# When the half-width sums of x are made in two MLP layers: beside the square products or inside the first quarter

## Chip, cores, metric

One core of a Trainium2 chip runs the whole program. The metric is device time in microseconds (us) of that core. The kernel before took 1035.24 us (median of 3 runs, 1034.46 to 1035.85).

## What is computed

The reference is an encoder of two layers on 512 tokens of width 1024, all in float32: a stick-breaking attention, then an MLP; a gated linear recurrence, then an MLP; a last norm. The change touches the two MLPs alone:

```
x = x + y                                  # behind the attention or the recurrence
h = rms_norm(x, norm_mlp[layer])
u = relu(h @ w1);  x = x + (u * u) @ w2    # w1: 1024 x 4096, w2: 4096 x 1024
```

## The kernel before, in words

Every float32 product is made of three products of halves: an operand is cast to a high half (`wh`, `xg`, `sh`, `bh`; a cast on ACT), and the low half (`wl`, `low`, `sl`, `bl`) is the difference, made on DVE. TensorE (PE) runs high by high, low by high and high by low.

An MLP works through the 4096 hidden features in four quarters of 1024. Quarter 0's first product is made plainly, as eight products of 24 matmuls (`squared(c)`, c from 0 to 7; this text calls them the square products). Everything else follows a scheme of seven products in place of eight on 2 x 2 blocks (`PRODUCTS`, P1 to P7): first the "down" step of quarter 0 (14 products, P1 0 to P4 1: name and half), then for the quarters 1 to 3 an "up" step and a "down" step of 14 products each. A loop in `run` goes through these products; `place(i)` numbers them in a cycle of 28, where 0 to 13 is up and 14 to 27 is down. Ahead of each product, `leave` reads the banks of the product before it (`collect`), and makes the halves of the weights for the product four further on (`prepare`: an addition on DVE or by an accumulating DMA from POOL, the cast `wh` on ACT, the difference `wl` on DVE).

The up steps need sums of blocks of x. With x cut into eight chunks, chunk k and chunk 4 + k make a pair (k from 0 to 3). Per pair, `sums_of_x(k)` scales both chunks by the norm's weights (two ACT instructions of 128x512) and makes four sums (four DVE instructions of 128x256, tile `x`); `halves_of_sums(k)` casts the halves (two ACT casts of 128x256 and one of 128x512) and takes the low halves (two DVE instructions of 128x256 and one of 128x512, tile `low`). So one pair is seven DVE and five ACT instructions. The first high half needs the place in `xgl` and the second the place in `xgh` that the plain x still occupies until the square products have used it. While that is so (`x_down` not yet called), a pair's two 128x256 casts go to a spare place (`bh` or `bl`, and `s3`), and `replace` copies them home later, two ACT casts per pair. A pair made later goes home directly.

What sets the order: PE's order is as written. Instructions of the other engines inside `run` keep the written order on ACT and on DVE (`Ordered`); those beside the square products are ordered by the framework's scheduler. Every engine takes its instructions in the order of its queue. Before, the first MLP made pairs 0 and 1 beside square products 4 and 5, pair 2 at the places 19 and 20, pair 3 at the places 24 and 25 of the first down step; the second MLP made pairs 0, 1, 2 beside the products 4, 5, 6 and pair 3 at the places 19 and 20. `replace` ran once, at place 21, for all pairs that lay aside. Helpers that record the order (line 776) stand for all of these instructions in the profile; the matmuls are at L236 to L238 (square products), L1107 (down) and L1012 (up).

Of the kernel before, what the change touches and what calls it, by code (L numbers as in the profile page):

```python
# [62 lines left out]
def hybrid_encoder(  # L63
# [40 lines left out]
    def f(ap):  # L104
        return ap.bitcast(F32)
# [28 lines left out]
    xgh, xgl = Chunks(0), Chunks(1)  # L134
# [629 lines left out]
    HS = S // 2  # L764
# [21 lines left out]
    class Mlp:  # L786
# [157 lines left out]
        def halves_of_sums(self, k):  # L944
# [14 lines left out]
            self.A.copy(self.s41[:, k, :], v)  # L959
            self.V.tensor_tensor(low, v, f(self.s41[:, k, :]), ALU.subtract)  # L960

        LOWER = {15: (0, 0), 16: (1, 0), 17: (0, 1), 18: (0, 2), 22: (1, 1), 23: (1, 2)}

        def lower(self, i, part):
# [14 lines left out]

        def replace(self):  # L980

            for k in list(self.s3):
                self.A.copy(xgh[:, k, HS:], f(self.s3[k]))
                here = self.s2(k)
                del self.s3[k]
                self.A.copy(self.s2(k), f(here))

        def slots_of(self, p):

# [154 lines left out]
        def run(self, first, between, end):  # L1144
# [13 lines left out]
            def place(i):  # L1158

                return (i + self.STEPS // 2) % self.STEPS  # L1160
# [8 lines left out]
            def add(i, ahead=1):  # L1169

                if i >= len(steps) or i in done or steps[i][3] not in ("P5", "P6"):
                    return
                *what, name = steps[i]
                far = what[0] == "down" and (name, what[2]) in FARS
                if ahead > (5 if far else 2 if name == "P5" else what[0] == "up"):
                    return
                if steps.index((*what, {"P5": "P1", "P6": "P5"}[name])) in made:
                    done.add(i)

                    self.added(unit(i), name, far=far)  # L1180
# [51 lines left out]
            def leave(i):  # L1232

                ahead = i + 4
                if i < 0:
                    return
                kind, q4, p, name = steps[i]
                bank = sums[kind, q4, p if kind == "up" else 0][self.PRODUCTS[name][3]]
                if kind == "down":
                    if q4 == 0 and place(i) == 21:  # L1240
                        self.replace()
                    if p:
                        self.collect(name, 0, bank[0])
                    if steps[min(ahead, len(steps) - 1)][0] == "down":
                        add(ahead, 0)
                    if p:
                        self.collect(name, 1, bank[1])
                    prepare(ahead)
                    if later and place(i) > 15:
                        later.pop()()  # L1250
                    if q4 == 0:
                        x_down(FRONT, ASIDE)
                        if place(i) in self.LOWER:
                            self.lower(*self.LOWER[place(i)])

                        k = ({19: 2, 20: 2, 24: 3, 25: 3}, {19: 3, 20: 3})[self.layer].get(place(i))
                        if k:
                            (self.sums_of_x if place(i) in (19, 24) else self.halves_of_sums)(k)
                    return
                u, three = us[p], bank.rearrange("p (i n) -> p i n", i=2)  # L1260
                keep = {"P1": 0, "P6": 1, "P5": 2, "P7": 3}.get(name)
                if keep is not None:

                    self.A.copy(u[keep], three)
                at, x, y, op = {
                    "P3": (1, three, u[1], ALU.subtract),
                    "P7": (2, u[2], u[3], ALU.subtract),
                    "P2": (0, u[0], three, ALU.add),
                    "P4": (3, three, None, None),
                }.get(name, (None,) * 4)  # L1270
                if op:
                    self.V.tensor_tensor(u[at], x, y, op)
                if name == "P4":
                    def fourth(u=u, three=three, p=p):
                        self.A.activation(u[3], three, AF.Relu)
                        self.square(u[3])
                        if p:
                            last_sums(u, self.SUMS[:2])
                        else:
                            self.sums(p, slice(0, 2))  # L1280

                    if p:
                        fourth()
                    else:
                        later.append(fourth)
                elif later:
                    later.pop()()
                prepare(ahead)
                if op:
                    def rest(u=u, at=at):  # L1290
                        self.A.activation(u[at], u[at], AF.Relu)
                        self.square(u[at])
                        if p:
                            self.split_slot(p, u[at], at)

                    if p and name == "P3":
                        later.append(rest)
                    else:
                        rest()
                    if name == "P2" and not p:  # L1300
                        self.split(p, slice(0, 2), slice(0, 3), slice(0, 3))
                elif name == "P4" and p:
                    last_sums(u, self.SUMS[2:3])
                    self.split_slot(p, u[2], 5)
                    later.append(lambda: last_sums(u, self.SUMS[3:]))
                    waiting[:] = [(p, u[j], 3 + j) for j in (0, 1, 3)]
                elif name in ("P5", "P6") and p:
                    n = ("P5", "P6").index(name)
                    self.split(0, n, slice(0, 4), slice(3, 7))
# [36 lines left out]
        def quarters(self, between, end):  # L1346
            for c in range(C - 1):
                self.squared(c)
                p, i = c // 4, c % 4 // 2
                if c % 2:  # L1350
                    self.split(p, i, slice(0, 3), slice(0, 3))
                    self.sums(p, i)
                    self.split(p, i, slice(0, 4), slice(3, 7))
                if c == 0:
                    units = self.from_down(0)
                    self.load(units, *self.FROM_UP)
                if c < 2:

                    for n in range(4 * c, 4 * c + 4):
                        self.sq.chunk(n, x[n], e=V)  # L1360
                if c == C - 2:
                    self.rr = self.sq.inv_squares(self.bank())
                between(c)

                k = c - 4
                if k in range(2 + self.layer):
                    with tc.issue_after(self.squares.ins):
                        self.sums_of_x(k)
                        self.halves_of_sums(k)
            self.run(units, between, end)  # L1370
            self.blocks.close()
# [460 lines left out]
```

## Time and profile before

| what | value |
|---|---|
| runs | 1034.46, 1035.24, 1035.85 us |
| the profiled execution's own time | 1034.89 us |
| its span in the profile | 1033.2 us |
| PE busy | 1022.3 us (99%) |
| DVE busy | 862.9 us (84%) |
| ACT busy | 713.5 us (69%) |
| granted PE clock | 0.999 |

The span is the time from the first to the last instruction in the profile; 1.7 us of the execution lie around it. Times below are us from the span's start. In a timeline row the first number is the start, the second the duration of the row (of all its instructions, where xN says more than one), then engine, line, operation, output<-input; what stands in brackets is the engine's idle time before the row and what ended it.

### The profile page before, as it was taken

The page shows a single profiled execution, that of the slowest core. Times are in us where ns is not written, and L with a number is a line of the kernel's source. Part 1 is how long each engine was busy: PE and PEld are TensorE (multiplying, and loading weights), DVE is VectorE, ACT ScalarE, POOL GpSimd, SP SyncE. Part 2 cuts the span into 40 slices and gives each one's busy share as a digit, 9 for nine tenths or more (in the row PEclk, how much of TensorE's full clock was granted, in tenths as well). Part 3 has the DMA queues.
Part 4 walks back from the last instruction along what each step waited for, and adds up shares of the span by engine and source line. Part 5 has one row for each costly group of instructions (what it writes and reads, how often), then busy time and mean ns, then how long its engine had stood idle before and what let it go on. Part 6 is the DMA issues. An engine that isn't in the chain of part 4 may idle for free.

```text
span 1033.2 us, 15885 instructions
## 1 busy us (share of the span) xinstructions
PE 1022.3 (99%) x5868; PEld 892.2 (86%) x5868; DVE 862.9 (84%) x1152; ACT 713.5 (69%) x1104; POOL 174.6 (17%) x235
## 2 busy tenths in 40 slices
PE   9999999999999999999999999999999999999997
PEld 7888888888888988988988888888888988988986
DVE  6988787847789699799799889984689899798898
ACT  6777676836778674774765689964777774874866
POOL 0444444420010010010011210300000010010012
PEclk9999999999999999999999999999999999999999
DMA  7745454537546667677683464452436677677663
GB/s 233 220 121 143 107 154 103 153 108 279 143 82 183 167 154 196 164 158 191 162 233 83 132 179 122 119 202 83 102 80 185 164 163 189 165 159 195 165 125 105
DMA packets 52700, 159.41 MB, mean 154 GB/s; under 512 B 6672, under 2 KB 7952, under 8 KB 52624
## 3 DMA queue, kind: packets, MB, share of 16 engines
q1 hardware_dynamic: 41376, 119.35, 35.8%
q0 software_dynamic: 10528, 38.28, 22.3%
q8 instruction: 46, 0.75, 0.3%
q10 hardware_dynamic: 720, 0.79, 0.2%
q14 instruction: 30, 0.25, 0.1%
HBM read 137.41 MB, written 4.19 MB: 137 GB/s over the span
## 4 chain that ended last, share of the span: by engine, by line
PE 89%; DVE 4%; ACT 3%; issue 2%; DMA 1%; POOL 0%; SPq 0%; DVEq 0%; ACTq 0%; POOLq 0%
PE ps_t L1107 13%; PE ps_acc L1012 8%; PE ps_z L1012 7%; PE ps_acc L1107 7%; PE ps_acc L236 5%; PE ps_acc L238 5%; PE ps_acc L237 5%; PE ps_o L1012 4%; PE ps_z L1107 3%; PE ps_t L236 3%; PE ps_t L237 3%; PE ps_t L238 3%; PE ps_o L236 2%; PE ps_o L237 2%; PE ps_o L238 2%
## 5 line engine op out<-in xcount | busy, mean ns | idle before, releaser
L776 ACT CAST wh<-b 128x1024 fp32r<-128x1024 f32 x168 | 174.1, 1050 | 112.5 <-DVE b L776 73.9
L776 DVE TENSOR_TENSOR wl<-b,wh 128x1024 fp32r<-128x1024 f32 x168 | 204.2, 1221 | 45.4 <-ACT wh L776 44.7
L1089 POOL DMA_DIRECT2D b<-in_w_dn x40 | 35.0, 876 | 352.0 <-DVE b L776 265.6
L236 PE MATMUL ps_acc<-xg,wh 128*128 128x512 f32 x200 | 81.6, 408 | 0.0
L1012 PE MATMUL ps_z<-xg,wh 128*128 128x256 f32 x384 | 79.0, 277 | 0.8 <-ACT u L776 0.8
L238 PE MATMUL ps_acc<-xg,wh 128*128 128x512 f32 x200 | 78.3, 392 | 0.0
L237 PE MATMUL ps_acc<-xg,wl 128*128 128x512 f32 x200 | 78.3, 391 | 0.0
L231 DVE TENSOR_TENSOR wl<-raw,wh 128x512 fp32r<-128x512 f32 (+2 forms) x70 | 62.2, 914 | 15.0 <-ACT wh L229 14.8
L600 DVE TENSOR_TENSOR_SCAN scan<-keep,later 128x128 f32<-128x128 f32 (+1 forms) x64 | 59.5, 933 | 16.2 <-ACT keep L590 9.9
L776 ACT ACTIVATE u<-u 128x512 f32<-128x512 f32 x100 | 63.1, 632 | 9.5 <-DVE u L776 7.7
L229 ACT CAST wh<-raw 128x512 fp32r<-128x512 f32 (+2 forms) x70 | 50.6, 758 | 23.9 <-PE ps_acc L238 7.3
L1012 PE MATMUL ps_z<-xg,wl 128*128 128x256 f32 x240 | 66.4, 277 | 0.0
L1012 PEld LDWEIGHTS ps_z<-xg,wh 128*128 128x128 f32 x384 | 62.8, 188 | 1.2 <-ACT u L776 1.0
L1012 PE MATMUL ps_acc<-xg,wh 128*128 128x256 f32 x288 | 61.6, 278 | 1.2 <-ACT u L776 1.2
L1089 POOL DMA_DIRECT2D b<-in_w_up x24 | 20.9, 870 | 241.8 <-DVE b L776 90.5
L604 POOL TENSOR_TENSOR w<-w,scan 128x128 f32<-128x128 f32 (+1 forms) x64 | 51.4, 805 | 54.4 <-DVE scan L600 51.4
L776 DVE TENSOR_TENSOR b<-b,b 128x1024 f32<-128x1024 f32 x48 | 58.7, 1224 | 1.3
L776 DVE TENSOR_TENSOR u<-u 128x512 f32<-128x512 f32 (+1 forms) x92 | 54.9, 597 | 2.6 <-ACT u L776 1.1
L1012 PE MATMUL ps_acc<-low,wh 128*128 128x256 f32 x192 | 53.2, 277 | 0.1
L1012 PE MATMUL ps_acc<-xg,wl 128*128 128x256 f32 x192 | 53.2, 277 | 0.0
L776 ACT CAST wh<-raw 128x1024 fp32r<-128x1024 f32 x46 | 48.0, 1045 | 6.9 <-PE ps_acc L1107 6.9
L1107 PE MATMUL ps_t<-wh,bh 128*128 128x512 f32 x126 | 49.4, 392 | 0.4 <-DVE c L776 0.4
(383 smaller groups left out, 3277.1 us busy)
## 6 DMA issues: line engine op xcount, KB each, us to landing
b<-in_w_dn SPq DMA_DIRECT2D x48, 512.0 KB, 4.6
b<-in_w_dn POOLq DMA_DIRECT2D x40, 512.0 KB, 5.5
b<-in_w_up SPq DMA_DIRECT2D x36, 512.0 KB, 4.6
b<-in_w_up POOLq DMA_DIRECT2D x24, 512.0 KB, 5.5
raw<-in_w_m SPq DMA_DIRECT2D x16, 512.0 KB, 4.3
raw<-in_w_dn SPq DMA_DIRECT2D x16, 512.0 KB, 4.6
raw<-in_w_in SPq DMA_DIRECT2D x16, 512.0 KB, 4.6
raw<-in_w_qk SPq DMA_DIRECT2D x12, 512.0 KB, 3.7
```

Source lines behind the costliest of these rows:

```text
L229: A.copy(wh[:, k, :], raw[:, k, :])
L231: V.tensor_tensor(wl[:, k, :], raw[:, k, :], f(wh[:, k, :]), ALU.subtract)
L236: PE.matmul(ps, wh, ah, start=start, stop=False)
L237: PE.matmul(ps, wl, ah, start=False, stop=False)
L238: PE.matmul(ps, wh, al, start=False, stop=stop)
L600: V.tensor_tensor_scan(sc[:, S - n : S][:, ::-1], keep[:, :n][:, ::-1], later[:, S - n :][:, ::-1], 1.0, ALU.mult, ALU.max,)
L604: G.tensor_tensor(wt, wt, sc[:, S - n + 1 : S + 1], ALU.mult)
L776: ins = getattr(self.e, name)(*args, **kwargs)
L1012: PE.matmul(ps[:, i * HS : (i + 1) * HS], m, y, start=new and i == k == n == 0, stop=i == 1 and k == C // 2 - 1 and n == 2, skip_group_che ...
L1089: G.dma_start(out=unit[b].rearrange("p j n -> p (j n)"), in_=unit["src"](to), accum_op=ALU.add)
L1107: PE.matmul(ps, m, y[:, jj, cols], start=first and n == 0, stop=last and n == 2, skip_group_check=not new,)
```

## The change

Three things move. In the first MLP pair 2 is made beside square product 6, and pair 3 takes over the places 19 and 20; the places 24 and 25 make none. In the second MLP pairs 0 and 1 are both made beside product 4, pair 2 beside product 5 and pair 3 beside product 6; the down step makes none. `replace` copies one pair at a time, at the places 19, 21, 24 and 25 while one lies aside: three pairs in the first MLP, four in the second, one more than before in each.

```diff
+        REPLACE = 19, 21, 24, 25
...
         def replace(self):
-            for k in list(self.s3):
-                self.A.copy(xgh[:, k, HS:], f(self.s3[k]))
-                here = self.s2(k)
-                del self.s3[k]
-                self.A.copy(self.s2(k), f(here))
+            k = min(self.s3)
+            here = self.s2(k)
+            self.A.copy(xgh[:, k, HS:], f(self.s3.pop(k)))
+            self.A.copy(self.s2(k), f(here))
...
-                    if q4 == 0 and place(i) == 21:
+                    if q4 == 0 and self.s3 and place(i) in self.REPLACE:
                         self.replace()
...
-                        k = ({19: 2, 20: 2, 24: 3, 25: 3}, {19: 3, 20: 3})[self.layer].get(place(i))
-                        if k:
-                            (self.sums_of_x if place(i) in (19, 24) else self.halves_of_sums)(k)
+                        if self.layer == 0 and place(i) in (19, 20):
+                            (self.sums_of_x, self.halves_of_sums)[place(i) - 19](3)
...
-                k = c - 4
-                if k in range(2 + self.layer):
+                for k in ({4: (0,), 5: (1,), 6: (2,)}, {4: (0, 1), 5: (2,), 6: (3,)})[self.layer].get(c, ()):
                     with tc.issue_after(self.squares.ins):
                         self.sums_of_x(k)
                         self.halves_of_sums(k)
```

Three places show how the queues change. The first is DVE in the first MLP, at the end of the first down step (`c_` are the collected outputs, `wl` low halves of weights, `b_` weight blocks, `x` and `low` the pair's sums and low halves). Before:

```order
L776 SCALAR_TENSOR_TENSOR c_3134<-ps_t,rr,c_3134 128x512 x2
L776 TENSOR_TENSOR wl<-b_3728,wh 128x1024
L776 TENSOR_TENSOR b_3728<-b_3728,b_3730 128x1024
L776 TENSOR_TENSOR x<-x 128x256 x4
L776 SCALAR_TENSOR_TENSOR c_3131<-ps_z,rr,c_3131 128x512 x2
L776 TENSOR_TENSOR wl<-b_3728,wh 128x1024
L776 TENSOR_TENSOR b_3728<-b_3728,b_3732 128x1024
L776 TENSOR_TENSOR low<-x,xg 128x256 x2
L776 TENSOR_TENSOR low<-x,s_3138 128x512
L776 TENSOR_TENSOR wl<-b_3728,wh 128x1024
```

The same place of the change:

```order
L776 SCALAR_TENSOR_TENSOR c_3134<-ps_t,rr,c_3134 128x512 x2
L776 TENSOR_TENSOR wl<-b_3745,wh 128x1024
L776 TENSOR_TENSOR b_3745<-b_3745,b_3747 128x1024
L776 SCALAR_TENSOR_TENSOR c_3131<-ps_z,rr,c_3131 128x512 x2
L776 TENSOR_TENSOR wl<-b_3745,wh 128x1024
L776 TENSOR_TENSOR b_3745<-b_3745,b_3749 128x1024
L776 TENSOR_TENSOR wl<-b_3745,wh 128x1024
```

The seven instructions of pair 3 have left the queue between the weights of the first up step.

The second place is ACT in the second MLP, from the end of the square products into the first down step (`sh` are high halves of the squares `u`, `s_` and `bl` places of the pairs' high halves, `ps_acc` the bank of square product 7). Before:

```order
L776 CAST sh<-u 128x1024
L776 CAST bl<-x 128x256
L776 CAST s_7356<-x 128x512
L776 ACTIVATE u<-ps_acc 128x512
L776 ACTIVATE u<-u 128x512
L776 CAST sh<-u 128x768
L776 CAST wh<-b_7427 128x1024
L776 CAST wh<-raw 128x1024
L776 CAST sh<-u 128x1024
L776 CAST wh<-b_7427 128x1024
```

The same place of the change:

```order
L776 ACTIVATE u<-ps_acc 128x512
L776 ACTIVATE u<-u 128x512
L776 CAST bl<-x 128x256
L776 CAST sh<-u 128x1024
L776 CAST sh<-u 128x768
L776 CAST wh<-b_7430 128x1024
L776 CAST wh<-raw 128x1024
L776 CAST s_7359<-x 128x512
L776 CAST sh<-u 128x1024
L776 CAST wh<-b_7430 128x1024
```

Before, `sh` and the two casts of pair 2 stood ahead of the reading of `ps_acc`; now `sh` and the same two casts of pair 3 stand behind it.

The third place is DVE in the second MLP, the same stretch. Before:

```order
L776 TENSOR_TENSOR sl<-u,sh 128x1024
L776 TENSOR_TENSOR low<-x,bl 128x256
L776 TENSOR_TENSOR low<-x,s_7356 128x512
L776 TENSOR_TENSOR sl<-u,sh 128x768
L776 TENSOR_TENSOR wl<-b_7427,wh 128x1024
L776 TENSOR_TENSOR u<-u 128x256 x4
L776 TENSOR_TENSOR wl<-raw,wh 128x1024
L776 TENSOR_TENSOR b_7427<-b_7427,b_7429 128x1024
L776 TENSOR_TENSOR sl<-u,sh 128x1024
L776 TENSOR_TENSOR wl<-b_7427,wh 128x1024
```

The same place of the change:

```order
L776 TENSOR_TENSOR sl<-u,sh 128x1024
L776 TENSOR_TENSOR sl<-u,sh 128x768
L776 TENSOR_TENSOR wl<-b_7430,wh 128x1024
L776 TENSOR_TENSOR u<-u 128x256
L776 TENSOR_TENSOR low<-x,s_7359 128x512
L776 TENSOR_TENSOR u<-u 128x256 x3
L776 TENSOR_TENSOR wl<-raw,wh 128x1024
L776 TENSOR_TENSOR b_7430<-b_7430,b_7432 128x1024
L776 TENSOR_TENSOR sl<-u,sh 128x1024
L776 TENSOR_TENSOR wl<-b_7430,wh 128x1024
```

The low halves that stood between the two `sl` now stand ahead of the first, and one 128x512 `low` has come in between the sums of `u`.

## The prediction

> **What bounds the kernel.** First the page's list of busy times, then the page of PE's waits.
>
> ```profile
> span 1033.2 us, 15885 instructions
> PE 1022.3 (99%) x5868; PEld 892.2 (86%) x5868; DVE 862.9 (84%) x1152; ACT 713.5 (69%) x1104; POOL 174.6 (17%) x235
> ...
> PE ps_acc L1012 <- ACT u L776: 1.2, 1, 1.2
> ...
> PE ps_z L1012 <- ACT u L776: 0.8, 1, 0.8
> ```
>
> PE sets the time: nothing that the change does to ACT or DVE counts unless PE waits less or more for it. The change leaves PE's instructions and their order as they are. Two of its few named waits are single events in an up step (L1012), for ACT. So I compare steps that have the same work, in the timeline of PE, by the starts of their first matmuls.
>
> ```profile
> 291.03 0.39 PE L1107 MATMUL ps_t<-wh,bh 128*128 128x512 f32 x1
> ...
> 329.93 0.28 PE L1012 MATMUL ps_acc<-xg,wh 128*128 128x256 f32 x1
> ...
> 371.65 0.39 PE L1107 MATMUL ps_t<-wh,bh 128*128 128x512 f32 x1
> ...
> 757.78 0.39 PE L1107 MATMUL ps_t<-wh,bh 128*128 128x512 f32 x1
> ...
> 796.80 0.28 PE L1012 MATMUL ps_acc<-xg,wh 128*128 128x256 f32 x1
> ...
> 834.98 0.39 PE L1107 MATMUL ps_t<-wh,bh 128*128 128x512 f32 x1
> ```
>
> L1107 to L1012 is the first down step, L1012 to L1107 the first up step. The up step takes 41.72 us in the first MLP (329.93 to 371.65) and 38.18 in the second (796.80 to 834.98), with the same matmuls. **3.54 us** are lost in the first MLP's alone, and the difference in work is that pair 3 is made there at the places 24 and 25, just ahead. The first down steps take 38.90 and 39.02 us.
>
> **Term 1: the first MLP's up step.** The timelines of DVE, POOL and ACT show the path of that loss.
>
> ```profile
> 327.23 1.79 DVE L776 TENSOR_TENSOR x<-x 128x256 f32<-128x256 f32 x4
> 328.94 1.40 DVE L776 SCALAR_TENSOR_TENSOR c<-ps_z,rr,c 128x512 f32<-128x512 f32 x2
> ...
> 332.65 0.75 DVE L776 TENSOR_TENSOR low<-x,xg 128x256 fp32r<-128x256 f32 x2
> 333.51 0.69 DVE L776 TENSOR_TENSOR low<-x,s 128x512 fp32r<-128x512 f32 x1
> 334.11 2.36 DVE L776 TENSOR_TENSOR wl<-b,wh 128x1024 fp32r<-128x1024 f32 x2
> ```
>
> ```profile
> 335.69 0.86 POOL L1089 DMA_DIRECT2D b<-in_w_up  x1 [6.93 <-DVE wl L776]
> ```
>
> ```profile
> 800.67 0.86 POOL L1089 DMA_DIRECT2D b<-in_w_up  x1 [5.00 <-DVE wl L776]
> ```
>
> ```profile
> 343.29 2.00 ACT L776 CAST wh<-b 128x1024 fp32r<-128x1024 f32 x2 [3.93 <-DMA b<-in_w_up]
> ```
>
> Pair 3 holds DVE from 327.23 to 328.94 and from 332.65 to 334.11: 3.17 us in front of the `wl` that has to be made before POOL may add to that block in place. POOL issues that addition 5.76 us after the step's first matmul (335.69 less 329.93), against 3.87 in the second MLP (800.67 less 796.80). ACT then stands idle for 3.93 us until it lands, with everything queued behind that cast: the next `wh`, the reading of the banks. Those are the 1.2 and 0.8 us for which PE waits. The change takes all seven DVE instructions away here. ACT gets two casts of pair 2 at place 24, against two scalings and three casts that go. Nothing else differs from the second MLP's step, so I take its 38.18 us: **-3.54 us**. The bounds are -2.0 (the two named waits alone) and -3.54.
>
> The load of x[7] back from memory waits for pair 3 and moves ahead with it on SP's queue. It stands there between loads of up weights and finds its chunk free by then; I count it at nothing, because the products that need those weights are a step away.
>
> **Term 2: the first MLP's first down step.** Pair 2 comes in beside product 6, and `replace` is spread. A pair costs DVE 3.17 us as above when each sum waits for the last. Between other instructions it costs less: two of 128x256 in 0.75 us means one every 0.34, the 128x512 holds the queue for 0.60 (333.51 to 334.11), so 6 x 0.34 + 0.60 = 2.64 us. The stretches it has to fit into, in the view by windows (PE, PEld, DVE, ACT, POOL busy):
>
> ```profile
> 285.60:301.00 15.40, 15.40 (x68) 12.70 (x69) 11.93 (x23) 9.55 (x14) 0.86 (x1) 1.00 0.11 27
> 743.60:767.60 24.00, 24.00 (x112) 19.97 (x111) 21.83 (x41) 18.17 (x30) 1.03 (x2) 1.00 0.26 56
> ```
>
> In the first MLP DVE has 15.40 - 11.93 = 3.47 us free, and ACT 5.85. The pair fits. In the queue of ACT the first collecting read of `ps_t` now stands ahead of an `sh` cast, where before it stood behind:
>
> ```profile
> 298.28 0.68 ACT L1121 ACTIVATE c<-ps_t,rr 128x512 f32<-128x512 f32 x1
> ```
>
> At most its 0.68 us is then in front of the weights of P5 1, for which PE waits at this place; bounds 0 and 0.7. The read comes only a little later than the cast before it ends anyway, so **+0.1 us**. The two copies at place 19 stand ahead of a weight cast, and two fewer stand at place 21: by then ACT has done the same four, so nothing is added there, and the extra two at place 24 fall into ACT's wait for DVE.
>
> **Term 3: the second MLP's first down step.** Here DVE has 24.00 - 21.83 = 2.17 us free for the same 2.64 to 3.17, and ACT's order is worse: reading product 7's bank now stands ahead of both an `sh` and a `bl` cast. I walk the queues from the end of product 7 on, with the old durations.
>
> ```profile
> 752.37 0.63 ACT L776 ACTIVATE u<-u 128x512 f32<-128x512 f32 x1
> 752.90 1.33 ACT L776 ACTIVATE x<-x,colt 128x512 f32<-128x512 f32 x2
> ...
> 756.37 1.05 ACT L776 CAST sh<-u 128x1024 fp32r<-128x1024 f32 x1
> 757.32 0.40 ACT L776 CAST bl<-x 128x256 fp32r<-128x256 f32 x1
> 757.62 0.62 ACT L776 CAST s<-x 128x512 fp32r<-128x512 f32 x1
> 758.14 0.59 ACT L776 ACTIVATE u<-ps_acc 128x512 f32<-128x512 f32 x1
> 758.76 0.63 ACT L776 ACTIVATE u<-u 128x512 f32<-128x512 f32 x1
> ```
>
> ```profile
> 757.45 1.23 DVE L776 TENSOR_TENSOR sl<-u,sh 128x1024 fp32r<-128x1024 f32 x1
> 758.59 0.42 DVE L776 TENSOR_TENSOR low<-x,bl 128x256 fp32r<-128x256 f32 x1
> ...
> 760.29 0.96 DVE L776 TENSOR_TENSOR sl<-u,sh 128x768 fp32r<-128x768 f32 x1 [0.49 <-ACT sh L776]
> 761.24 1.23 DVE L776 TENSOR_TENSOR wl<-b,wh 128x1024 fp32r<-128x1024 f32 x1
> 762.38 1.80 DVE L776 TENSOR_TENSOR u<-u 128x256 f32<-128x256 f32 x4
> 764.10 1.22 DVE L776 TENSOR_TENSOR wl<-raw,wh 128x1024 fp32r<-128x1024 f32 x1
> 765.23 1.22 DVE L776 TENSOR_TENSOR b<-b,b 128x1024 f32<-128x1024 f32 x1
> ...
> 767.62 2.36 DVE L776 TENSOR_TENSOR wl<-b,wh 128x1024 fp32r<-128x1024 f32 x2
> ```
>
> ```profile
> 768.90 0.50 PE L1107 MATMUL ps_acc<-wl,sh 128*128 128x512 f32 x1
> ```
>
> Product 7's last matmul ends at about 757.95, where the next product has started (757.78). ACT: reading the bank, 0.62 to the next start (758.14 to 758.76); the square, 0.53 (752.37 to 752.90); `bl`, 0.30 (757.32 to 757.62); so `sh` starts at 759.40 and ends 1.05 later, 760.45. DVE: `sl` 1.14 (757.45 to 758.59), `sl` 0.95 (760.29 to 761.24), `wl` 1.14 (761.24 to 762.38), so the sums of `u` begin at 763.7, not 762.38. Up to `wl<-raw` they take 1.72 (762.38 to 764.10) and 0.48 more for the `low` between them (0.60, and the 0.34 before it in place of 0.46). From there to the last `wl`, by way of the addition and ACT's cast, it is 3.52 as before (764.10 to 767.62). That `wl` starts at 763.7 + 2.20 + 3.52 = 769.4, not at 767.62: 1.8 us later. It is the weight of P5 1, and the PE row above starts within 0.1 us of its end: PE has no slack there. So **+1.8 us**; the bounds are 0.5 (2.64 less 2.17, all holes used) and 3.17 (none used).
>
> The Trainium skill, "VectorE: DVE Perf Modes", section "The DRAIN you can't avoid", says that the next DVE instruction does not start until the pipe of the one before is empty. By it, the six spacings on DVE in this walk would be full durations, some 0.1 us longer each; the sum would be worse by about 0.5 us, near 1033.5. The rows speak against it (`low` starts at 758.59, 0.09 ahead of the end of `sl`, and two `low` fit in 0.75), as does that page's later section, "Two Vector instructions with no wait between them", by which an instruction that isn't held starts earlier.
>
> Behind this point the second MLP gains: no pair is made at the places 19 and 20 any more. PE's row at the end of that step shows what its seven DVE instructions cost:
>
> ```profile
> 791.24 0.47 PE L1107 MATMUL ps_t<-wh,bh 128*128 128x512 f32 x1 [0.23 <-DVE c L776]
> ```
>
> With the wait, the matmul's stretched time (0.47, against 0.39) and the same in the one before it, that is about 0.5 us, and some 0.1 in smaller places. All DVE work behind place 20 is 3.17 us earlier relative to PE, far more than this lateness: **-0.6 us**. Eight copies instead of six stand on ACT, two of them at each of four places; ACT has room there for 0.6 each.
>
> **The sum** against the profiled execution (1034.89 us: 1033.2 span and 1.7 around it): -3.54 + 0.1 + 1.8 - 0.6 = -2.2, so 1032.7. The median of the three runs is 0.35 higher than that execution: **1033.0 us**.
>
> **Rivals.**
>
> *The second MLP hides its pair.* If the holes of 2.17 us can be used nearly in full and ACT reads product 7's bank without holding back `sh`, term 3 is 0.5 and the sum -3.5: 1031.7. For it speaks that ACT has 5.8 us free in that stretch; against it, that the walk begins at PE's own end of product 7, which no hole can move. Chance 0.13.
>
> *The up step is relieved only in part.* The accumulating DMA shares its time with loads that SP issues; if it lands late again, ACT's wait shrinks by the 1.9 us by which it is issued earlier, but the second wait (0.8 us and its stretched neighbours, 1.1) stays. Then term 1 is -2.4 and the result 1034.1. Trainium skill, "DMA: Bandwidth & Descriptors", section "Issuing engines are not separate DMA queues": DMAs of all issuers run on the same 16 engines and interleave. This trace cannot separate them, but the same additions land in the second MLP beside the same loads and PE doesn't wait. Chance 0.15. The same time comes out if term 3 is at its upper bound of 3.17 (1034.4): another 0.12.
>
> *Slower: the pair's own chain runs in series.* A pair goes back and forth between ACT and DVE: two scalings (1.33), four sums (1.79), the casts (0.40, 0.40, 0.62), the lows (0.75, 0.69): 6.0 us if the two in-order queues wait for each other at every step. Less the holes this is 6.0 - 3.47 = 2.5 us in the first MLP and 6.0 - 2.17 = 3.8 in the second, and PE waits for both: -3.54 + 2.5 + 3.8 - 0.6 = +2.2, so 1037.4. It decides once the pair takes DVE more than its free time in the two stretches, with DVE idle inside the pair. Against it: the scheduler has put a pair's steps between other instructions. Chance 0.11.
>
> **How the numbers follow.** The forecast has 0.49, with its own range of 1031.9 to 1034.1. A measurement of this kernel can tell about 0.2% from no change, 2.07 us: below 1033.17 is faster, above 1037.3 slower. The forecast lies right at the first line, so I give 0.30 of its chance to faster and 0.19 to the same; the first rival is faster, the partial ones the same, and the last slower. Together: faster 0.43, same 0.46, slower 0.11. The range leaves out the slower rival and little below: 1031.3 to 1035.6.
>
> **What would show it.** Right: the first MLP's up step at 38.2 us and ACT's idle time of 3.93 us before that cast gone; the second MLP's first down step at about 40.2 us, with a PE wait of about 1.8 us at the matmul `ps_acc<-wl,sh` for DVE `wl`; no wait for DVE `c` at that step's end. Wrong: an up step over 39 us, or a down step in the first MLP over 39.5; PE waits beside the square products, where it has none now, would mean that the pair in series is the case.

## The result, and the profile after

The changed kernel takes **1033.39 us** (median of 15 runs, 1031.86 to 1034.14), against 1034.84 us for the kernel before on the same chips (15 runs, 1034.46 to 1039.22). The ratio is 0.9978, with a 95% interval of 0.9970 to 0.9986: 1.4 to 3.1 us faster. The medians lie 1.45 us apart; the ratio agrees with that of the means, which gives 2.2 us, and one run of 1039.22 makes 0.3 us of it. The forecast was 1033.0, or 2.2 us faster. The profiled execution took 1033.58 us.

The page's first lines, and then the page of PE's waits, of the changed kernel:

```profile
span 1031.9 us, 15893 instructions
...
PE 1022.2 (99%) x5868; PEld 892.6 (87%) x5868; DVE 862.0 (84%) x1152; ACT 715.8 (69%) x1108; POOL 169.8 (16%) x235
```

```profile
PE ps_acc L1107 <- DVE wl L776: 0.7, 2, 0.5
...
PE ps_z L1107 <- DVE wl L776: 0.3, 1, 0.3
PE ps_t L1107 <- DVE c L776: 0.3, 1, 0.3
...
PE ps_t L1107 <- DVE wl L776: 0.2, 1, 0.2
```

The two waits of 1.2 and 0.8 us for ACT in the up step (L1012) have left the list, and new ones for `wl` in a down step (L1107) have come. The starts of the same steps as before, in PE's timeline:

```profile
291.83 0.39 PE L1107 MATMUL ps_t<-wh,bh 128*128 128x512 f32 x1
...
330.92 0.28 PE L1012 MATMUL ps_acc<-xg,wh 128*128 128x256 f32 x1
...
369.31 0.39 PE L1107 MATMUL ps_t<-wh,bh 128*128 128x512 f32 x1
...
755.25 0.39 PE L1107 MATMUL ps_t<-wh,bh 128*128 128x512 f32 x1
...
795.39 0.28 PE L1012 MATMUL ps_acc<-xg,wh 128*128 128x256 f32 x1
...
833.56 0.39 PE L1107 MATMUL ps_t<-wh,bh 128*128 128x512 f32 x1
```

| step | before | after | difference | forecast |
|---|---|---|---|---|
| first MLP, first down | 38.90 | 39.09 | +0.19 | +0.1 |
| first MLP, first up | 41.72 | 38.39 | -3.33 | -3.54 |
| second MLP, first down | 39.02 | 40.14 | +1.12 | +1.8 - 0.6 |
| second MLP, first up | 38.18 | 38.17 | -0.01 | 0 |

The steps add up to -2.03. The two profiled executions differ by 1.31 only, mainly because the first MLP's down step begins 0.80 later after the change (291.83 for 291.03). It begins between 290.1 and 292.9 in the traces of this study, and the differences arise ahead of 250 us, in the attention, which no kernel here changes. So the steps below are compared within the traces, and the times only where they differ by more than this.

### The profile page after: what moved, and what is told of

Same layout as the page of the kernel before. It is cut to its first block, busy times and chain, and to the rows that moved or that the text cites. A ratio compares the mean times of both kernels' runs of the same rounds, so it can differ in the third digit from the quotient of the medians.

```text
span 1031.9 us, 15893 instructions
## 1 busy us (share of the span) xinstructions
PE 1022.2 (99%) x5868; PEld 892.6 (87%) x5868; DVE 862.0 (84%) x1152; ACT 715.8 (69%) x1108; POOL 169.8 (16%) x235
## 4 chain that ended last, share of the span: by engine, by line
PE 90%; DVE 4%; ACT 3%; DMA 2%; issue 1%; SPq 0%; ACTq 0%; DVEq 0%
PE ps_t L1107 15%; PE ps_acc L1012 10%; PE ps_z L1012 8%; PE ps_acc L1107 7%; PE ps_acc L236 5%; PE ps_acc L238 5%; PE ps_acc L237 5%; PE ps_o L1012 5%; PE ps_z L1107 4%; PE ps_t L237 2%; PE ps_t L236 2%; PE ps_t L238 2%; PE ps_o L236 2%; PE ps_o L237 2%; PE ps_o L238 2%; PE ps_t L622 2%
## 5 line engine op out<-in xcount | busy, mean ns | idle before, releaser
L1012 PE MATMUL ps_z<-xg,wh 128*128 128x256 f32 x384 | 78.7, 277 | 0.0
L1012 PE MATMUL ps_z<-xg,wl 128*128 128x256 f32 x240 | 66.3, 276 | 0.0
L1012 PEld LDWEIGHTS ps_z<-xg,wh 128*128 128x128 f32 x384 | 62.8, 188 | 0.1
L1012 PE MATMUL ps_acc<-xg,wh 128*128 128x256 f32 x288 | 61.4, 277 | 0.0
L1012 PE MATMUL ps_acc<-xg,wl 128*128 128x256 f32 x192 | 53.1, 276 | 0.0
L1012 PE MATMUL ps_acc<-low,wh 128*128 128x256 f32 x192 | 53.0, 276 | 0.0
L1107 PE MATMUL ps_t<-wh,bh 128*128 128x512 f32 x126 | 49.2, 390 | 0.3 <-DVE c L776 0.3
```

The source lines that it names most:

```text
L1012: PE.matmul(ps[:, i * HS : (i + 1) * HS], m, y, start=new and i == k == n == 0, stop=i == 1 and k == C // 2 - 1 and n == 2, skip_group_che ...
L1107: PE.matmul(ps, m, y[:, jj, cols], start=first and n == 0, stop=last and n == 2, skip_group_check=not new,)
```

## Where the first MLP's gain comes from

The rows of POOL and ACT after the change, and the duration of the DMA (the last number, from issue to landing), after and then before:

```profile
334.71 0.86 POOL L1089 DMA_DIRECT2D b<-in_w_up  x1 [4.96 <-DVE wl L776]
```

```profile
340.94 2.17 ACT L776 CAST wh<-b 128x1024 fp32r<-128x1024 f32 x2 [1.02 <-DMA b<-in_w_up]
```

```profile
b<-in_w_dn SPq DMA_DIRECT2D x2, 512.0 KB, 5.3
b<-in_w_up POOLq DMA_DIRECT2D x1, 512.0 KB, 6.1
raw<-in_w_dn SPq DMA_DIRECT2D x1, 512.0 KB, 4.7
```

```profile
b<-in_w_dn SPq DMA_DIRECT2D x2, 512.0 KB, 6.6
b<-in_w_up POOLq DMA_DIRECT2D x1, 512.0 KB, 7.5
raw<-in_w_dn SPq DMA_DIRECT2D x1, 512.0 KB, 6.2
```

POOL issues the addition 3.79 us into the up step, for 5.76 before: 1.97 earlier. The addition itself is 1.4 us shorter. Together that is 3.34 at ACT's cast, which starts 10.02 us into the step, for 13.36 before, and the step is 3.33 shorter. The path to this DMA was in the prediction; that the DMA's own duration would change was not. Four experiments take this path apart.

### DVE's work put back: `dve_work_back`

```diff
                         if self.layer == 0 and place(i) in (19, 20):
                             (self.sums_of_x, self.halves_of_sums)[place(i) - 19](3)
+                        if self.layer == 0 and place(i) in (24, 25):
+                            for n, at in enumerate(((0, HS), (HS, S)) * 2 if place(i) == 24 else ((0, HS), (HS, S), (0, S))):
+                                t = self.lows[n % 3][:, slice(*at)]
+                                self.V.tensor_tensor(t, f(t), f(t), ALU.max)
```

> The changed kernel, with seven DVE instructions put back at the places 24 and 25 of the first MLP, of the widths that pair 3's had there (six of 128x256, one of 128x512), each writing the maximum of a low part with itself in place. No ACT work comes with them, and x[7] and x[3] are loaded back as early as in the changed kernel. My theory, DVE's 3.17 us in front of wl: the up step goes back from 38.4 to about 41.7 us, ACT waits near 3.9 us for the block that POOL adds to, and the time is 3.3 us above that of the changed kernel. The rival, by which the gain comes from the earlier load or from ACT's scalings and casts: the up step stays at 38.4 us.

DVE's, POOL's and ACT's rows of that run:

```profile
328.10 1.43 DVE L776 TENSOR_TENSOR low<-low 128x256 fp32r<-128x256 f32 x4
329.44 1.40 DVE L776 SCALAR_TENSOR_TENSOR c<-ps_z,rr,c 128x512 f32<-128x512 f32 x2
...
333.15 1.36 DVE L776 TENSOR_TENSOR low<-low 128x256 fp32r<-128x256 f32 x3
334.42 2.35 DVE L776 TENSOR_TENSOR wl<-b,wh 128x1024 fp32r<-128x1024 f32 x2
```

```profile
336.00 0.86 POOL L1089 DMA_DIRECT2D b<-in_w_up  x1 [6.36 <-DVE wl L776]
```

```profile
343.56 2.00 ACT L776 CAST wh<-b 128x1024 fp32r<-128x1024 f32 x2 [3.72 <-DMA b<-in_w_up]
```

The up step is back at 41.08 us: 2.69 of the 3.33 return with seven DVE instructions of other data, and with them ACT's wait (3.72). The instructions stand 2.61 us in front of `wl` (1.34 and 1.27, from their start to the next row's); pair 3's stood there for 3.17, and some of its sums need the result of an earlier one. The issue is 1.38 later than in the changed kernel (336.00, with the step's start at 330.83: 5.17), and the DMA takes 7.5 us again. 1035.82 us, ratio to the kernel before 1.0005 (0.9996 to 1.0014), where 1036.7 was expected. So DVE's work alone brings the loss back; the load of x[7] is issued as early as in the changed kernel (319.68, 11.1 us ahead of the step, in both), so its place is not the cause.

### All of the pair's work put back: `pair_work_back`

```diff
+                            for n in range(2) if place(i) == 24 else ():
+                                self.A.copy(at(n, ab), f(at(n, ab)))
...
+                                if place(i) == 25: self.A.copy(t, f(t))
```

> The changed kernel with pair 3's whole work put back at the first MLP's places 24 and 25: the seven DVE instructions of the run before, and five ACT instructions of the old widths ahead of them (two of 128x512, two of 128x256 and one of 128x512, copies of low parts in place). The load of x[7] stays early. DVE's work alone brought the up step to 41.08 us, 0.64 below the 41.72 of the kernel before. Theory: ACT's work and its back and forth with DVE make up the rest, so 41.6 to 42.2 us. The rival, by which the rest is the place of the load: 41.1 us.

41.44 us, between the two. The addition is issued at the same 5.17, so ACT's five instructions delay no issue; its DMA takes 7.8 us instead of 7.5, which is all of the 0.36 us to a tenth. Whether ACT's work has to do with it, this run cannot say: the same step takes 40.68, 41.72 and 42.12 us in three executions with the old arrangement (table below), so both runs with work put back lie within that spread. 1035.68 us (1.0011, 1.0002 to 1.0020).

### The load of x[7] put back late: `load_late`

```diff
+        def hold(self, c):
+            self.V.tensor_tensor(x[c][:, :1], x[c][:, :1], x[c][:, :1], ALU.max)
...
+                        if self.layer == 0 and place(i) == 25:
+                            self.hold(7)
```

> The changed kernel with one DVE instruction on a single column of x[7] at the first MLP's place 25, so that x[7] comes free late and its load from memory stands where it stood before, behind the loads of all six up blocks and with the accumulating DMA. Nothing else of pair 3's work comes back. My theory, in which the load's place costs nothing: the up step stays at 38.4 us, at most 0.2 above. The rival, by which the load's place makes up the 0.64 us that DVE's work alone did not bring back: 39.0 us.

```profile
333.34 0.86 POOL L1090 DMA_DIRECT2D b<-in_w_up  x1 [4.95 <-DVE wl L776]
```

```profile
339.54 2.24 ACT L776 CAST wh<-b 128x1024 fp32r<-128x1024 f32 x2 [0.94 <-DMA b<-in_w_up]
```

The step is 38.30 us (329.60 to 367.90), the DMA 6.1: a late load costs nothing here. It is not quite in its old place, though. It is issued 1.15 us into the step (330.75) and has landed 0.3 us after the addition is issued; in the kernel before it was issued 4.30 us into the step (334.23) and ran beside the addition for 1.2 us. That an overlap isn't needed for the loss, the two runs before show, in which the load is early and the step long. 1032.71 us (0.9982, 0.9973 to 0.9990).

### The same pair in the second MLP: `second_at_24`

```diff
-k = ({19: 2, 20: 2, 24: 3, 25: 3}, {19: 3, 20: 3})[self.layer].get(place(i))
+k = ({19: 2, 20: 2, 24: 3, 25: 3}, {24: 3, 25: 3})[self.layer].get(place(i))
```

This is the kernel before with one number pair changed.

> The kernel before, with pair 3 of the second MLP moved from the places 19 and 20 to 24 and 25, where the first MLP has it. My theory, that a pair at 24 and 25 holds back the block that POOL adds to: the second MLP's first up step goes from 38.2 to about 41.7 us as in the first, the collecting wait of its first down step (0.23 us) goes and takes 0.2 to 0.5 us with it, and the time is 3.0 to 3.4 us above that of the kernel before. The rival, that the first MLP's loss comes from something that only that MLP has (its loads back from memory, its first collecting reads on ACT): the second's up step stays at 38.2 us.

```profile
800.83 0.87 POOL L1089 DMA_DIRECT2D b<-in_w_up  x1 [6.91 <-DVE wl L776]
```

```profile
807.73 2.00 ACT L776 CAST wh<-b 128x1024 fp32r<-128x1024 f32 x2 [1.95 <-DMA b<-in_w_up]
```

A miss in size: the second MLP's up step goes to 39.32 only (+1.14), its down step to 38.38 (-0.64), and the time is the same (1034.29 us, 0.9998, 0.9989 to 1.0007). The expectation overlooked that this edit adds no pair to the second MLP's down step. It moves one there, from the places 19 and 20. The moment at which POOL issues the addition, counted from the up step's first matmul, follows the number of pairs made in the down step ahead more than their place:

| pairs in the first down step | trace and MLP | issued at |
|---|---|---|
| none | after, second | 2.13 |
| one, at 19 and 20 | after, first | 3.79 |
| one, at 19 and 20 | before, second | 3.87 |
| one, at 24 and 25 | second_at_24, second | 4.05 |
| two | before, first | 5.76 |

(The down step of the first row is the one that has PE's new waits early in it.) So in the first MLP the change took one pair of two out of that step, and the issue came 1.97 earlier; here it moved by 0.18 only. Most of what this step lost is the DMA's duration, in the kernel before and then in this run:

```profile
b<-in_w_up POOLq DMA_DIRECT2D x1, 512.0 KB, 5.4
```

```profile
b<-in_w_up POOLq DMA_DIRECT2D x1, 512.0 KB, 6.8
```

That puts ACT's cast at 10.95 us into the step, for 9.37, and part of these 1.58 us costs nothing, because the second MLP has some room.

How much room, all the traces say together. ACT's cast that waits for the addition, from the step's first matmul, beside the step's length:

| trace and MLP | cast starts at | up step | step less cast |
|---|---|---|---|
| before, first | 13.36 | 41.72 | 28.36 |
| second_mlp_only, first | 13.76 | 42.12 | 28.36 |
| second_at_24, first | 12.33 | 40.68 | 28.35 |
| dve_work_back, first | 12.73 | 41.08 | 28.35 |
| pair_work_back, first | 13.08 | 41.44 | 28.36 |
| all_together, first | 10.34 | 38.70 | 28.36 |
| after, first | 10.02 | 38.39 | 28.37 |
| load_late, first | 9.94 | 38.30 | 28.36 |
| second_at_24, second | 10.95 | 39.32 | 28.37 |
| before, second | 9.37 | 38.18 | 28.81 |

In nearly all traces the step ends 28.36 us behind that cast, to 0.02, where the cast starts later than about 9.8 us into it, and takes 38.18 otherwise. The four traces with other orders or amounts in the second MLP, described in the next part, agree (28.35 to 28.38). `first_mlp_only` and `first_and_together` do not: with casts at 9.91 and 9.87 it is 28.68 and 28.67, and the following down step is 0.3 shorter; that is left open.

The addition's DMA, 6.0 to 7.9 us in the first MLP, is the other half of where the cast stands. The three traces with pair 3 at 24 and 25 of the first MLP issue it at 5.72 to 5.76 and get it after 6.5, 7.5 and 7.9 us: 1.4 us of difference between executions of the same instructions. In the nine traces with one pair in that down step and nothing put back behind it, it takes 6.0 to 6.5. So the gain of this change is no fixed number. The up step takes 40.68 to 42.12 us in the three and 38.30 to 38.70 in the nine: between 2.0 and 3.8 us, and 3.0 by the means.

## Where the second MLP's loss comes from

ACT, DVE and PE of the changed kernel, in the stretch that the prediction walked:

```profile
755.45 0.60 ACT L776 ACTIVATE u<-ps_acc 128x512 f32<-128x512 f32 x1 [1.02 <-PE ps_acc L238]
756.08 0.63 ACT L776 ACTIVATE u<-u 128x512 f32<-128x512 f32 x1
756.62 0.39 ACT L776 CAST bl<-x 128x256 fp32r<-128x256 f32 x1
756.92 1.78 ACT L776 CAST sh<-u 128x1024 fp32r<-128x1024 f32 x2
```

```profile
757.05 0.43 DVE L776 TENSOR_TENSOR low<-x,bl 128x256 fp32r<-128x256 f32 x1 [0.83 <-ACT bl L776]
758.00 2.09 DVE L776 TENSOR_TENSOR sl<-u,sh 128x1024 fp32r<-128x1024 f32 x2 [0.52 <-ACT sh L776]
760.01 1.22 DVE L776 TENSOR_TENSOR wl<-b,wh 128x1024 fp32r<-128x1024 f32 x1
...
763.33 1.22 DVE L776 TENSOR_TENSOR wl<-raw,wh 128x1024 fp32r<-128x1024 f32 x1
...
766.87 1.23 DVE L776 TENSOR_TENSOR wl<-b,wh 128x1024 fp32r<-128x1024 f32 x1
```

```profile
761.28 0.50 PE L1107 MATMUL ps_t<-wl,sh 128*128 128x512 f32 x1 [0.20 <-DVE wl L776]
...
764.61 0.50 PE L1107 MATMUL ps_z<-wl,bh 128*128 128x512 f32 x1 [0.27 <-DVE wl L776]
...
768.15 0.50 PE L1107 MATMUL ps_acc<-wl,sh 128*128 128x512 f32 x1 [0.53 <-DVE wl L776]
```

The walk's last `wl` was to start at 769.4, or 11.62 us into the step; it starts at 766.87, or 11.62. The first `sh` ends at 757.97 (2.72 into the step; walk 2.67). `wl<-raw` starts at 8.08 (walk 8.12). PE loses 1.0 us in the three waits, and the rest, about 0.8, in the longer matmuls behind them (0.50 and 0.40, for 0.39): 1.8 as forecast (the step is 1.76 longer than the 38.38 of `second_at_24`), but at three products (P1 1, P2 0, P5 1), where the text had one wait at P5 1. P1 1 and P2 0 had less slack than it allowed.

### The second MLP alone: `second_mlp_only`

```diff
-k = ({19: 2, 20: 2, 24: 3, 25: 3}, {19: 3, 20: 3})[self.layer].get(place(i))
+k = ({19: 2, 20: 2, 24: 3, 25: 3}, {})[self.layer].get(place(i))
...
-                k = c - 4
-                if k in range(2 + self.layer):
+                for k in ({4: (0,), 5: (1,)}, {4: (0, 1), 5: (2,), 6: (3,)})[self.layer].get(c, ()):
```

> The change in the second MLP alone; the first MLP is as in the kernel before. My theory: slower than the kernel before by the 1.1 us that the traces show in the second MLP's first down step (39.02 to 40.14), so about 1036.0; the first MLP's up step stays at 41.7 us. The rival, by which the second MLP's pair is hidden and the two traces differ there by chance, gives no difference from the kernel before.

The second MLP's down step is 40.12 us and the first MLP's up step 42.12. 1035.80 us, ratio 1.0008 (0.9999 to 1.0017): slower by 0.6 us with an interval that just takes in nothing. The step is 40.10 to 40.15 in all five traces with this arrangement.

The least that this step took is 38.38 us, in `second_at_24`, where pair 3 is made at the end of the step and three pairs beside the products 4 to 6, as in the kernel before. Measured by it, pair 3 at 19 and 20 had cost 0.64 (39.02), and a fourth pair beside the products 4 to 6 costs 1.76 (40.14). The terms of the prediction were 0.6 and 1.8. Both arrangements have a pair beside product 6, so it is the fourth pair in all that costs; whether another way of dividing the four among these products would be cheaper, no run here tried.

### ACT's order: `cast_before_bank`

```diff
-            self.A.copy(h, u)
+            self.cast = self.A.copy(h, u)
...
-            self.A.activation(t, ps.rearrange("p (h n) -> p h n", h=2), AF.Relu)
+            behind = self.layer and c == C - 1
+            with tc.issue_after(self.cast.ins) if behind else nullcontext():
+                self.A.activation(t, ps.rearrange("p (h n) -> p h n", h=2), AF.Relu)
```

> The changed kernel, with one order more: in the second MLP, ACT reads the last square product's bank only after the sh cast of 1024 columns, so that bl and sh need not wait for the end of that product. The pair's work stays where it is. My theory, that the loss begins at ACT's reading of the bank: DVE's two holes of 0.83 and 0.52 us go, the first down step falls from 40.1 to about 38.9 us, and the time is 1.2 us below that of the changed kernel. The rival, DVE's amount of work (2.64 us of it for 2.17 us that were free): the step loses at most 0.4 us, since DVE is as full as before.

```profile
756.01 1.23 DVE L776 TENSOR_TENSOR sl<-u,sh 128x1024 fp32r<-128x1024 f32 x1
757.15 0.69 DVE L776 TENSOR_TENSOR low<-x,s 128x512 fp32r<-128x512 f32 x1
758.41 0.96 DVE L776 TENSOR_TENSOR sl<-u,sh 128x768 fp32r<-128x768 f32 x1 [0.57 <-ACT sh L776]
759.36 1.23 DVE L776 TENSOR_TENSOR wl<-b,wh 128x1024 fp32r<-128x1024 f32 x1
```

39.66 us: 0.48 gained, not 1.2. The step begins at 754.61, so the first `sl` comes at 1.40 instead of 2.75, but a new hole (0.57, for the second `sh`, behind the reading and the square on ACT) gives most of it back: `wl` starts 4.75 into the step, and had started at 4.76. What is gained comes behind that, where one `low` no longer stands. That is nearer to the rival: of the loss, ACT's reading of the bank by itself makes this half us. 1032.09 us (0.9971, 0.9961 to 0.9981).

### DVE's amount: `sums_short`, and both: `short_and_cast`

```diff
-            lo, hi = slice(0, HS), slice(HS, S)
+            n = 32 if (self.layer, k) == (1, 3) else HS
+            lo, hi = slice(0, n), slice(HS, HS + n)
```

> The changed kernel, in which the second MLP's four sums of pair 3 are made on 32 columns of their 256, so that the rest of that pair's numbers is left out. ACT still reads the last square product's bank ahead of the sh cast. Theory now, after the order of ACT alone gave back 0.5 of the step's us: DVE is full up to that bank's reading, so its amount of work sets when the sums of u and the sh cast come. About 1 us of DVE work less then takes 0.7 to 1.1 us from the second MLP's first down step (40.14 to about 39.2 us). The rival, my first walk, in which only ACT's order counts: the step stays within 0.2 us of 40.14.

39.70 us: 0.44 gained, between the two. DVE now stands idle for 1.1 and 0.5 us at the same place, waiting for ACT's `bl` and `sh` behind the bank. The edit did one thing more than its text says: with the shorter sums the scheduler also put the square of that bank (`u<-u`) behind `sh` on ACT, so the 0.44 is not DVE's amount alone. 1032.51 us (0.9980, 0.9971 to 0.9989). So I took both away:

> The changed kernel with both edits that gave half each: in the second MLP, ACT reads the last square product's bank only after the sh cast, and pair 3's four sums are made on 32 of their 256 columns (the rest of that pair's numbers is left out). Theory now: the sh cast has two waits side by side, for DVE to come to the sums of u (DVE full) and for ACT's place behind the bank's reading (that product's end); taking either away leaves the other, which is why each gave 0.45 us. Both together then give more than their sum of 0.9: the first down step at 38.6 us, about where it would be without any loss and without the collecting wait. The rival, by which each is worth its half on its own: 39.2 us.

38.96 us: 1.18 gained, more than the sum of the two (0.92) and less than the 1.5 expected; 0.6 above the 38.38 of `second_at_24` stay, and are not explained. ACT's order here is that of `cast_before_bank`, so between these two only DVE's amount differs, and it is worth 0.70 us. A gain above the sum fits an `sh` that waits for the later of two things, DVE's sums of `u` and the end of product 7, though part of each is worth something by itself. 1031.87 us (0.9970, 0.9959 to 0.9980).

### What PE needs first: `urgent_first`

```diff
-                    with tc.issue_after(self.squares.ins):
+                    with tc.issue_after((self.cast if (self.layer, k) == (1, 3) else self.squares).ins):
```

It has the edit of `cast_before_bank` too.

> The changed kernel with all of its work, in another order in the second MLP: pair 3's work beside product 6 goes behind the sh cast of 1024 columns, so that DVE makes the sums of u first, and ACT reads the last square product's bank behind that cast as well. If the loss is one of order (what PE waits for stands behind what it doesn't), the first down step is at 39.0 to 39.3 us with pair 3 still there; if it is one of amount (2.64 us of DVE for 2.17 that were free, plus the sums that then wait for each other), it stays at 39.6 us as with the reading alone.

```profile
754.95 1.23 DVE L776 TENSOR_TENSOR sl<-u,sh 128x1024 fp32r<-128x1024 f32 x1 [1.12 <-ACT sh L776]
756.19 1.34 DVE L776 TENSOR_TENSOR x<-x 128x256 f32<-128x256 f32 x3
...
763.08 1.22 DVE L776 TENSOR_TENSOR wl<-raw,wh 128x1024 fp32r<-128x1024 f32 x1
```

40.84 us: worse by 0.70 than the changed kernel. The first `sl` comes early (0.64 into the step, which starts at 754.31), but DVE idles 1.12 us ahead of it, since the pair may not begin, and then the pair's work stands in front of `wl<-raw` (8.77 into the step, for 8.08). What this order takes from ahead of `sh` comes back ahead of the weights. Neither expectation (39.0 to 39.3, or 39.6) holds: that of amount is nearer, and this order even costs. 1033.57 us (0.9988, 0.9979 to 0.9997).

## The copies, one pair at a time

### The first MLP alone: `first_mlp_only` and `first_and_together`

```diff
-for k in ({4: (0,), 5: (1,), 6: (2,)}, {4: (0, 1), 5: (2,), 6: (3,)})[self.layer].get(c, ()):
+for k in {4: (0,), 5: (1,), 6: (2,)}.get(c, ()):
...
-if self.layer == 0 and place(i) in (19, 20):
+if place(i) in (19, 20):
```

> The change in the first MLP alone; the second MLP is as in the kernel before. My theory: the two halves of the change are independent, so the first MLP's first up step is at 38.4 us as after the change, the second MLP's first down step is back at 39.0 us (40.14 after the change), and the time is 1.1 us below that of the changed kernel, about 1032.0 to 1032.3. The rival is that the second MLP's 1.1 us come from something else than its pair 3 (a state that the first MLP leaves): then the step stays at 40.1 us and the time is that of the changed kernel.

The first MLP's up step is 38.59, but the second's down step 39.67 us, neither 39.0 nor 40.1. PE, ACT and DVE:

```profile
779.60 0.47 PE L1107 MATMUL ps_t<-wh,bh 128*128 128x512 f32 x1 [0.49 <-DVE c L776]
```

```profile
774.05 0.41 ACT L776 CAST xg<-s 128x256 fp32r<-128x256 f32 x1
774.36 0.41 ACT L776 CAST xg<-bh 128x256 fp32r<-128x256 f32 x1
774.67 1.05 ACT L776 CAST wh<-b 128x1024 fp32r<-128x1024 f32 x1
```

```profile
776.99 1.80 DVE L776 TENSOR_TENSOR x<-x 128x256 f32<-128x256 f32 x4
778.71 1.40 DVE L776 SCALAR_TENSOR_TENSOR c<-ps_t,rr,c 128x512 f32<-128x512 f32 x2
```

Two copies (0.62 us) now stand ahead of the `wh` cast at place 19; pair 3's sums follow it, and behind them the collecting `c` that frees a bank. 1031.86 us (0.9968, 0.9955 to 0.9980). To test this, the second MLP's copies went back to place 21:

```diff
-                    if q4 == 0 and self.s3 and place(i) in self.REPLACE:
+                    while q4 == 0 and self.s3 and place(i) in (self.REPLACE, (21,))[self.layer]:
                         self.replace()
+                        if not self.layer: break
```

> As the kernel with the change in the first MLP alone, but the second MLP copies all laid-aside halves together at place 21 again, as the kernel before does. In the run with the change in the first MLP alone the second MLP's first down step took 39.67 us, with a wait of 0.50 us for a collecting c where the kernel before has none. Theory: the two copies at place 19 stand ahead of ACT's weight cast there and make DVE late by 0.6 us, and pair 3's sums stand right behind; without them the step is back at 39.0 us and the time at about 1031.2 us, the fastest so far. The rival, by which that wait has another cause (the first MLP's buffers, or chance): the step stays at 39.7 us.

39.05 us: right, the copies at 19 cost 0.62. The time is 1031.76 us (0.9972, 0.9961 to 0.9982), not the 1031.2 expected; against the 1031.86 of `first_mlp_only` it does not show these 0.6 us.

### All copies together: `all_together`

```diff
-                    if q4 == 0 and self.s3 and place(i) in self.REPLACE:
+                    while q4 == 0 and self.s3 and place(i) == 21:
```

> As the kernel with the change in the first MLP and all copies of the second MLP's halves at place 21, but the first MLP too copies all its halves at place 21, so that the splitting of the copies is undone everywhere and only the pairs have moved. Theory: the first MLP has pair 3 at the places 19 and 20 as the second has, and the two copies at 19 hold back DVE there as they did in the second; the wait of 0.25 us for a collecting c at the end of that step stays, and the step is at 38.9 to 39.1 us, so the splitting is worth nothing or up to 0.2 us against it. The rival, by which six copies on one spot hold back the next weights: 39.3 us or more.

The rival was right: the first MLP's down step is 39.70 us, 0.61 longer than with the copies apart. Its PE row, and the same matmul in the changed kernel:

```profile
326.20 0.47 PE L1107 MATMUL ps_t<-wh,bh 128*128 128x512 f32 x1 [0.88 <-DVE c L776]
```

```profile
325.39 0.47 PE L1107 MATMUL ps_t<-wh,bh 128*128 128x512 f32 x1 [0.26 <-DVE c L776]
```

Six copies on one spot put the `wh<-raw` cast 0.62 us later (27.46 against 26.84 into the step), and the `c` behind it. DVE waits there for that cast:

```profile
320.58 1.23 DVE L776 TENSOR_TENSOR wl<-raw,wh 128x1024 fp32r<-128x1024 f32 x1 [1.24 <-ACT wh L776]
```

In the second MLP of `first_and_together`, with pair 3 and six copies at the same places, the same `wl` starts without any idle time before it (782.40): DVE is the later of the two engines there. A likely reason, not tested, is that ACT reads `ps_t` for 1.25 us ahead of the copies in the first MLP (314.42 in `all_together`), and DVE does so in the second. So the same edit, copies one by one, is worth 0.6 us in the first MLP and costs 0.6 in the second, with pair 3 at 19 and 20 in both. 1032.71 us (0.9980, 0.9971 to 0.9989).

By the three steps of the table, `first_and_together` is the best version: 39.09 + 38.54 + 39.05 = 116.68 us, against 117.62 after the change and 119.64 before. By the times it is faster than the kernel before; from the changed kernel it cannot be told apart (0.9972 and 0.9978, with intervals that overlap).

## Why the prediction held

- **Term 1 (-3.54) came as -3.33**, by the path it named: DVE, the addition's issue, ACT's idle time. ACT's idle time did not go, but fell from 3.93 to 1.02; the remaining 0.2 us is that cast, at 10.02 instead of 9.8. The step assumed the second MLP's value as the floor, and the floor was right (38.18). What it did not account for is the way from an issue 1.9 us earlier to a step 3.54 us shorter: 1.97 us are the issue, and 1.4 a shorter DMA. That the size came out so near is luck in part. The term rests on one execution's 41.72, and by the spread above the gain could have been anything from 2.0 to 3.8 us, 3.0 by the means. The rival "relieved only in part" took the DMA's sharing as a danger to the gain; a shorter DMA made up two fifths of it. The Trainium skill, "DMA: Bandwidth & Descriptors", section "Issuing engines are not separate DMA queues", says that DMAs of all issuers run on the same engines. The trace fits that: beside the late addition SP's loads of the same size are longer as well (6.6 and 6.2 us before, 5.3 and 4.7 after).
- **Term 2 (+0.1) came as +0.19**, with a wait of 0.20 us for `wl` at P5 1 (it had been 0.03). That the split copies cost nothing is right, and hides a second fact: together they would have cost 0.6.
- **Term 3 (+1.8 and -0.6) came as +1.76 and -0.64** by the floor of 38.38. The walk was exact at its end; one wait became three. Its path, that all begins with ACT's reading of the bank, is only part of it (0.48 us by itself): DVE's full queue is the other (0.70 once ACT's order is out of the way), and they overlap.
- **The Trainium skill's rule** ("VectorE: DVE Perf Modes", section "The DRAIN you can't avoid") would have put the walk's last `wl` about 0.5 us later than 11.62. It starts at 11.62: the trace does not agree, for instructions that wait for nothing, which is the exception that the prediction named.
- The slower rival, a pair in series beside the square products, did not come: PE has no wait there in any of these traces.

## What to carry to other kernels

Compare like steps within one trace, and look for the DMA in the chain: a step whose length follows one transfer's landing one for one (here 28.36 us behind the cast that waits for it, in nine rows of the table) names its bound better than any list of waits. Work that is taken off the path of a DMA's issue can gain more than the issue moves (here 1.97 us at the issue and 3.34 at the cast behind the landing), because the DMA's duration changes too; and that part varies from one execution to the next, so a forecast from one trace needs a range for it. When an edit moves work instead of adding it, count what stood there before: the miss of `second_at_24` came from this. Small copies have no fixed price: the same 0.6 us was a gain in one layer and a loss in the other, by which engine was the later one where the copies stood.

## What the runs showed of the hardware

A 512 KB addition in place, issued by POOL at the same point of the same work, took 6.5, 7.5 and 7.9 us in three executions beside three loads of 512 KB from SP, and 6.0 to 6.5 us in the nine traces in which it was issued 2 us earlier. I had taken it for fixed. The loads beside it are an argued reason: in the three, SP issues the second load 3.2 us behind the addition (before: 338.88 and 335.69), in the changed kernel 4.7 us behind it (339.43 and 334.71). They are not the whole of it. In the second MLP the addition took 5.4 us before and 6.8 in `second_at_24`, with the loads issued within 0.2 us of the same distances (2.1, 4.6 and 5.8 us behind it, and 2.1, 4.5 and 5.6). No run here took the loads away, and the cause stays open.
